# Block inverses of a gated DeltaNet layer: their TensorE products in four pieces, head products planned in pieces of two channel blocks

## The chip, the cores and the metric

The kernel runs on one core of one Trainium2 chip. The metric is the time of one execution in microseconds (us), lower is better; a row of times gives the median of several executions.

## What is computed

A two-layer backbone over 512 latent tokens and 256 context tokens of width 1024, in float32. Layer 0 is a bidirectional gated DeltaNet, layer 1 a grouped-query attention with axial rotary angles. The change lies in layer 0 alone. Its reference, cut to what matters here:

```python
p = u @ w_in                                    # u: normed and modulated tokens
qkv = silu(centred_dwconv(p[..., :4096], conv_w))   # 8 q heads, 8 k heads, 16 v heads of 128
...                                             # q and k l2-normalised; beta = sigmoid, g = log-decay
# per head and direction, in chunks of 64 tokens:
a = where(strict, einsum('bhncd,bhnsd->bhncs', kb, kc) * decay, 0)
t_inv = triangular_solve(eye + a, eye, left_side=True, lower=True, unit_diagonal=True)
u = t_inv @ vb;  w = t_inv @ (kb * exp(gc))
def step(s, xs):                                # scan over the chunks
    v_new = u_i - w_i @ s
    o = qd_i @ s + qk_i @ v_new
    s = s * gl_i + kd_i^T @ v_new
```

## The kernel before

Layer 0 has two stages that matter here. In the first, TensorE (PE) makes the projections of the heads and, between them, the chunk matrices; in the second it runs the scan over twelve steps.

*Head products.* The first stage handles 40 column blocks of `w_in` in the order of `heads` ("qz" eight times, then "vvz" eight times), 128 columns each. Each block is a weight tile of 8 channel blocks (`KT`) of 128x128, split into a high and a low float32r half (`high` on ScalarE, `low` on GpSimd or VectorE). `products_of(n_, part)` makes 24 matmuls for one block: 8 channel blocks by three passes (high weight by high input, high by low, low by high), into one PSUM bank `g`; part 0 has the 512 latent tokens, part 1 the 256 context tokens. These matmuls are line 752 (756 after the change). VectorE and ScalarE then make the convolution and the SiLU of each part.

*Chunk matrices.* Tokens are kept as six pairs of chunks, t = 0 to 5. For each t the plan holds: `masked_nodes` (matrix of k with itself, masked and decayed, PE line 948); `solve_nodes`, in which GpSimd (POOL) inverts the 32x32 diagonal blocks of two t at once in 31 steps (lines 1051, 1052, and 1055 at the end); `join_nodes`, which joins two 32x32 inverses to one 64x64 inverse; and `query_nodes` (q by k, PE line 1014, masked, decayed by POOL on line 634, stored to `qk_d`).

*The join, for one t.* VectorE transposes the solved blocks into two tiles `U0` and `U1` (line 1073). `first` makes 64 float32 matmuls of 32x32 by 32 columns into the PSUM tile `pp` (line 1080). `negated` copies `pp` with a minus sign over `mo` on ScalarE (line 1083). `second` makes 64 more such matmuls into `pw` (line 1090). Eight copies `gathered` (`Tt` from `U`) and four copies `placed` (`Tt` from `pw`) fill a 1 MB tile `Tt`, which is stored to `t_d` (line 1111). Each of the 64 matmuls shows as two MATMUL and two LDWEIGHTS records in the profile, so a burst is "x128".

*What sets the order.* Every piece of work is a `Node` with an engine ("T" is TensorE, "V" VectorE, "S" ScalarE, "G" GpSimd, "D" a transfer or a delay), a cost, a rank, the nodes it depends on (`deps`), and the buffers that it takes with those that free them (`takes`, sizes in `RINGS`). `in_order` takes, again and again, the node that can start first by its own clock of each engine, and of several the one of lowest rank. The nodes are then run in that order, and each engine executes its own instructions in just that order. A "T" node depending on another engine's node is placed at least `LAG["T"]` = 1.0 after it; on a "D" node no engine clock acts. Transfers are issued on SyncE's queue (SP) in order as well.

*Loads of the scan's first step.* At the end of the list, `first_kq`, `first_v`, `first_T`, `first_QK` and `first_kt` load what step 0 reads: `ckq` (line 605), `cv` (1155), `cT` (1161), `cQK` (1167, 1169) and `ckt` (1180); after the change these lines are 605, 1177, 1183, 1189, 1191 and 1202. `cT`, `cQK` and `ckt` take the three tiles `df` that the decays used. The loads of the next steps (same tile names, other numbers) stand behind them on SP. In the scan, `products` makes `ks` (PE line 1460; VectorE's `r` on line 1463 reads `ks` and `cv`), `solve` makes `pr` from `r` and `cT` (1485), `update` makes `pq` from `cQK` (1507) and `su` from `ckt` (1515).

Of the kernel before, what the change touches and what calls it, by code (L numbers as in the profile page):

```python
# [8 lines left out]
F32 = mybir.dt.float32  # L9
# [8 lines left out]
P = 128  # L18
D = 1024
KT = 8  # L20
NLAT, NCTX = 512, 256
NTOK = NLAT + NCTX
NT = 6
QH, VH = 8, 16
# [73 lines left out]
def backbone(tc, a, out):  # L98
    nc = tc.nc
    V, S, G, T = nc.vector, nc.scalar, nc.gpsimd, nc.tensor  # L100
# [93 lines left out]
    pa = psA.__enter__()  # L194
# [281 lines left out]
    p2, p5 = gemm_T(None, None, 64, "ab")  # L476
# [187 lines left out]
    def node(engine, cost, rank, fn, *deps, takes=()):  # L664

        x = Node(engine, cost, rank, fn, deps, list(takes))
        nodes.append(x)
        return x
# [73 lines left out]
        weights[n_][2] = ap_.tile([P, KT, P], F32R, tag="wl", name=f"wl_{n_}", bufs=3)  # L742
        (G if n_ < EARLY else V).tensor_tensor(weights[n_][2], weights[n_][0], weights[n_][1], ALU.subtract)  # L743

    def products_of(n_, part):

        c0, n = parts[part]
        w, wh, wl = weights[n_]
        ps = pa.tile([P, 512], F32, tag="g", name=f"g{n}_{n_}", bufs=4)
        for k in range(KT):  # L750
            for m, (w_, u) in enumerate(((wh, uh), (wh, ul), (wl, uh))):
                T.matmul(ps[:, :n], w_[:, k], u[:, k, c0:c0 + n], start=k == 0 and m == 0, stop=k == KT - 1 and m == 2)  # L752
        sums[n_, part] = ps

    def taken(n_, part):

# [92 lines left out]
    for n_, (f_, h) in enumerate(heads):  # L849
# [4 lines left out]
        lw = node("D", 0.0 if first else 5.5, n_, go(load_weights, n_))  # L854
        hi = node("S", 0.0 if first else 1.06, n_ + 0.5, go(high, n_), lw)
        lo = node("G" if n_ < EARLY else "V", 0.0 if first else 2.5 if n_ < EARLY else 1.6, n_ + 0.5, go(low, n_), hi)
        for part in range(2):
            p[part] = node("T", (5.48, 2.92)[part], n_, go(products_of, n_, part), lo, p[0], *before)
            before = [p[part]]
        lw.takes.append(("w", [lo]))  # L860
        hi.takes.append(("wh", [p[1]]))
        lo.takes.append(("wl", [p[1]]))
        for part in range(2):
            if f_ == "z":
                th = node("S", (0.62, 0.4)[part], n_, go(tanh_of, n_, part), p[part], s_[0])
                s_[part] = node("V", (0.69, 0.42)[part], n_, go(silu_of, n_, part), th)
                if part == 0:
                    alloc = th
            else:
                x = first_ = node("S", (0.7, 0.48)[part], n_, go(taken, n_, part), p[part], acc0 if part else None)  # L870
                if part == 0:
                    acc0 = x
                for j in (0, 1, 3, 4):
                    x = node("V", (0.75, 0.49)[part], n_, go(spread, n_, part, j), x)
                th = node("S", (0.62, 0.4)[part], n_, go(tanh_of, n_, part), x)
                s_[part] = node("V", ((0.83, 0.56) if f_ == "q" else (0.69, 0.42))[part], n_, go(silu_of, n_, part), th, s_[0])
                if part == 0:
                    alloc = s_[0]
            p[part].takes.append(("g", [s_[part]]))
        if f_ != "z":  # L880
            acc0.takes.append(("acc", [s_[1]]))
        if f_ == "v":
# [181 lines left out]
    def join_nodes(t, rank):  # L1064
# [7 lines left out]
            U = box[d] = tl.tile([P, 2, VH, 32], F32, tag=f"U{d}", name=f"U{d}" + nm)  # L1072
            V.transpose(U.rearrange("p v h j -> p j (v h)"), X if d == 0 else X.rearrange("p i j -> p j i"))

        def first():
            box["pp"] = pp = pa.tile([P, VH, 32], F32, tag="gq", name="pp" + nm)
            for h in range(VH):
                for b in range(4):
                    i0, o0, d = b * 32, (b ^ 1) * 32, 1 - b % 2
                    T.matmul(pp[o0:o0 + 32, h, :], mos[t][i0:i0 + 32, h, :], box[d][i0:i0 + 32, of(b, d), h, :], start=True, stop=True, tile_position=(i0, o0))  # L1080
# [1 line left out]
        def negated():  # L1082
            S.activation(mos[t], box["pp"], AF.Copy, scale=-1.0)

        def second():
            box["pw"] = pw = pa.tile([P, VH, 32], F32, tag="gq", name="pw" + nm)
            for h in range(VH):
                for b in range(4):
                    i0 = b * 32
                    T.matmul(pw[i0:i0 + 32, h, :], box[1 - b % 2][i0:i0 + 32, of(b, b % 2), h, :], mos[t][i0:i0 + 32, h, :], start=True, stop=True, tile_position=(i0, i0))  # L1090
# [8 lines left out]
        def placed(b):  # L1099
            c0 = 32 - (b % 2) * 32  # L1100
            S.copy(Tt[b * 32:b * 32 + 32, of(b, b % 2), :, c0:c0 + 32], box["pw"][b * 32:b * 32 + 32])

        us = []
        for d in range(2):
            us.append(node("V", 2.15, rank, lambda d=d: turned(d), solved[t], before_U.get(t), *us))
        p1 = node("T", 1.32, 0, first, *us)
        sn = node("S", 0.61, rank - 0.5, negated, p1)
        p2 = node("T", 1.32, 0, second, sn)
        gs = [node("S" if t < LATE else "G", 0.62 if t < LATE else 1.1, rank, lambda b=b, d=d: gathered(b, d), us[d], cleared) for d in range(2) for b in range(4)]
        pl = [node("S", 0.58, rank - 0.5, lambda b=b: placed(b), p2) for b in range(4)]  # L1110
        st_ = node("D", 6.0, rank, lambda: dma(t_d[t], Tt), *gs, *pl)
        p1.takes.append(("gq", [sn]))
        p2.takes.append(("gq", pl))
        us[0].takes.append(("U", gs + [p2]))
# [5 lines left out]
        u_done[t], second_done[t] = us, p2  # L1120

    def clear():

# [1261 lines left out]
```

## Time and profile before

| what | value |
|---|---|
| median of 3 executions | 1182.38 us (1180.96 to 1186.59) |
| the profiled execution, its own time | 1193.88 us |
| its span (first to last instruction) | 1192.1 us, 28134 instructions |
| PE busy | 1134.5 us, 95% |
| VectorE, ScalarE, GpSimd busy | 836.9, 705.8 and 631.4 us |
| head products, line 752 | 222.0 + 217.7 + 217.1 us over 1920 matmuls |
| `pp` and `pw` matmuls | 768 records each, 192 ns median |
| first `pp`, last `pw` | 349.5 and 561.3 us |
| scan, first `ks` | 565.14 us |

The profiled execution took 11.5 us more than the median of the ordinary ones. Times in the trace are us from the span's start. A row of a timeline gives the start, the duration, the engine and line, the output and inputs, and in brackets the idle time before it with what ended it. Durations of matmuls include their way through the array, so the spacing of starts is what one costs in a stream. "issue" is time in which the engine waited for nothing that the profile shows.

### The profile page before, as it was taken

The numbers are of one execution on the slowest core, as the hardware profiler recorded it, in microseconds if no ns is written. First come the engines' busy times: TensorE is split into PE (matmuls) and PEld (weight loads), VectorE is DVE, ScalarE is ACT, GpSimd is POOL, SyncE is SP. The second block draws the span as 40 slices with busy tenths as digits, with TensorE's granted clock in tenths as the row PEclk, the third lists the DMA queues.
The fourth block names the chain that finished last, engine by engine and source line by source line (L and its number), as shares of the span: only waits on it lengthen the run. The fifth ranks groups of instructions, "written<-read, shape, count | busy, mean of one in ns | idle before, by whom it ended". The sixth has DMA issues, their size and how long they took to land.

```text
span 1192.1 us, 28134 instructions
## 1 busy us (share of the span) xinstructions
PE 1134.5 (95%) x10779; PEld 921.5 (77%) x10779; DVE 836.9 (70%) x1842; ACT 705.8 (59%) x1831; POOL 631.4 (53%) x515
## 2 busy tenths in 40 slices
PE   3999999999998999999999999999998989999996
PEld 1777678888887888888566666788886878989885
DVE  2498664778889687777678888687667866556536
ACT  5544344677666668655779888653533246666632
POOL 0031014329999899793575598557663043153531
PEclk9999999999999999999999999999999999999999
DMA  9478977555646585785988856576743021121133
GB/s 320 167 229 243 305 238 207 152 170 143 175 118 206 186 237 176 238 255 172 276 225 243 248 155 172 169 228 191 234 159 124 1 71 36 37 71 37 40 131 77
DMA packets 166104, 204.56 MB, mean 172 GB/s; under 512 B 13489, under 2 KB 115026, under 8 KB 165202
## 3 DMA queue, kind: packets, MB, share of 16 engines
q1 hardware_dynamic: 159170, 199.13, 55.0%
q10 hardware_dynamic: 6800, 3.64, 1.0%
q8 instruction: 85, 1.39, 0.5%
q14 instruction: 49, 0.40, 0.1%
HBM read 161.96 MB, written 40.67 MB: 170 GB/s over the span
## 4 chain that ended last, share of the span: by engine, by line
PE 82%; DVE 6%; DMA 6%; ACT 2%; issue 2%; SPq 1%; POOL 1%; ACTq 0%; DVEq 0%; POOLq 0%
PE g L752 29%; PE po L1385 11%; PE ks L1460 6%; PE pg L2026 3%; PE pg L1980 3%; PE g_k L414 3%; PE po L2094 2%; DMA aw<-in_ada_w 2%; PE kv L1833 2%; PE su L1515 2%; PE s L2044 2%; PE pso L2327 2%; PE pr L1485 2%; PE pa L245 1%; PE pt L2072 1%
## 5 line engine op out<-in xcount | busy, mean ns | idle before, releaser
L752 PE MATMUL g<-uh,wh 128*128 128x512 f32 (+1 forms) x640 | 222.0, 347 | 0.0
L752 PE MATMUL g<-ul,wh 128*128 128x512 f32 (+1 forms) x640 | 217.7, 340 | 3.9 <-issue 3.9
L752 PE MATMUL g<-uh,wl 128*128 128x512 f32 (+1 forms) x640 | 217.1, 339 | 0.0
L769 DVE SCALAR_TENSOR_TENSOR acc<-g,cwv,acc 128x510 f32<-128x510 f32 (+1 forms) x192 | 117.0, 614 | 43.7 <-ACT acc L761 39.2
L752 PEld LDWEIGHTS g<-uh,wl 128*128 128x128 f32 x640 | 122.8, 192 | 17.4 <-issue 4.2
L752 PEld LDWEIGHTS g<-uh,wh 128*128 128x128 f32 x640 | 122.8, 192 | 14.6 <-issue 1.1
L752 PEld LDWEIGHTS g<-ul,wh 128*128 128x128 f32 x640 | 123.0, 192 | 12.5 <-issue 0.5
L1385 PE MATMUL po<-woh,y 128*128 128x512 f32 x384 | 127.7, 400 | 0.0
L1468 POOL TENSOR_TENSOR S<-S,glb 128x512 f32<-128x512 f32 x88 | 89.9, 1041 | 58.1 <-PE ks L1460 58.1
L1052 POOL TENSOR_TENSOR X<-X,tmp 128x62 f32<-128x62 f32 (+15 forms) x93 | 95.6, 1028 | 7.3
L1051 POOL TENSOR_TENSOR tmp<-L,X 128x62 f32<-128x62 f32 (+15 forms) x93 | 94.6, 1018 | 6.4
L1460 PE MATMUL ks<-S,ckq 128*64 128x256 f32 x768 | 93.5, 386 | 2.3 <-ACT O L1465 2.2
L1385 PEld LDWEIGHTS po<-woh,y 128*128 128x128 f32 x384 | 72.2, 188 | 14.8 <-issue 0.2
L1460 PEld LDWEIGHTS ks<-S,ckq 128*64 128x64 f32 x768 | 51.1, 137 | 41.5 <-ACT O L1465 10.4
L1328 POOL TENSOR_TENSOR wol<-wo,woh 128x512 fp32r<-128x512 f32 (+1 forms) x32 | 52.6, 1643 | 56.2 <-ACT woh L1319 25.5
L1385 PE MATMUL po<-wol,y 128*128 128x512 f32 x192 | 75.1, 391 | 0.0
L743 POOL TENSOR_TENSOR wl<-w,wh 128x1024 fp32r<-128x1024 f32 x11 | 26.4, 2399 | 90.5 <-ACT wh L738 72.8
L211 POOL TENSOR_TENSOR wl_k<-w_k,wh_k 128x1024 fp32r<-128x1024 f32 x8 | 19.0, 2386 | 99.2 <-ACT wh_k L210 99.2
L761 ACT ACTIVATE acc<-g,cwv 128x512 f32<-128x512 f32 (+1 forms) x48 | 27.9, 581 | 64.2 <-PE g L752 63.7
L2075 DVE TENSOR_TENSOR pT<-pt,pT 128x384 fp32r<-128x384 f32 x64 | 33.4, 554 | 45.4 <-ACT pT L2074 45.4
L1463 DVE SCALAR_TENSOR_TENSOR r<-ks,negV,cv 128x128 f32<-128x128 f32 x192 | 56.6, 345 | 7.2 <-PE ks L1460 3.6
L1533 DVE TENSOR_TENSOR S<-su,S 128x512 f32<-128x512 f32 x88 | 56.6, 685 | 5.7 <-PE su L1515 3.9
(416 smaller groups left out, 2887.8 us busy)
## 6 DMA issues: line engine op xcount, KB each, us to landing
aw<-in_ada_w SPq DMA_DIRECT2D x24, 1024.0 KB, 7.5
w<-in_dn_w_in SPq DMA_DIRECT2D x40, 512.0 KB, 4.9
wo<-in_dn_w_out SPq DMA_DIRECT2D x32, 512.0 KB, 3.9
cv<-v_d SPq DMA_DIRECT2D x80, 128.0 KB, 5.5
df<-gc_d SPq DMA_DIRECT2D x48, 128.0 KB, 3.5
z_d<-sil SPq DMA_DIRECT2D x16, 384.0 KB, 4.3
v_d<-vt SPq DMA_DIRECT2D x16, 384.0 KB, 4.2
t_d<-Tt SPq DMA_DIRECT2D x6, 1024.0 KB, 4.7
```

The lines of the kernel that those rows point to most:

```text
L414: mm = T.matmul(pg_[:m, :n], w[:, k, :m], u[:, k, c0:c0 + n], start=k == 0 and n_ == 0, stop=k == KT - 1 and n_ == 2)
L752: T.matmul(ps[:, :n], w_[:, k], u[:, k, c0:c0 + n], start=k == 0 and m == 0, stop=k == KT - 1 and m == 2)
L769: V.scalar_tensor_tensor(a_[:, c0 + lo:c0 + hi], ps[:, lo + j - 2:hi + j - 2], cwv[:, j, ct:ct + 1], a_[:, c0 + lo:c0 + hi], ALU.mult, ALU ...
L1051: G.tensor_tensor(tv, bcast(L[:, :, j + 1:, j], 3, j + 1), bcast(X[:, :, j, 0:j + 1], 2, n), ALU.mult)
L1052: G.tensor_tensor(X[:, :, j + 1:, 0:j + 1], X[:, :, j + 1:, 0:j + 1], tv, ALU.subtract)
L1328: G.tensor_tensor(wl[:, :c], w[:, :c], wh[:, :c], ALU.subtract)
L1385: T.matmul(acc[j][nh], y[i][:, j, :], ww[k][:, nh * 512:(nh + 1) * 512], start=h == 0 and x == 0, stop=h == VH - 1 and x == 2)
L1460: T.matmul(ks[r0:r0 + 64, w], kq[:, w, slot(hh), r0:r0 + 64], St[hh][:, d], start=True, stop=True)
L1463: V.scalar_tensor_tensor(r[:, 2 * j + i], ks[:, 0, i], negV[:, visit, t, h0 + i:h0 + i + 1], v[:, 2 * hh + i], ALU.mult, ALU.add)
L1468: G.tensor_tensor(St[hh], St[hh], bcast(g_, 3, P), ALU.mult)
L1533: V.tensor_tensor(St[hh], raw(sj, 0, [[512 - 1024 * j, 2], [P, 2], [1, P]]), St[hh], ALU.add)
L1980: T.matmul(pgq, uL[i][:, k, t * P:(t + 1) * P], wq[j][:, k], start=k == 0 and n_ == 0, stop=k == KT - 1 and n_ == 2)
```

## The change

`products_of` is planned in four pieces per part, two channel blocks each (six matmuls), so that other "T" nodes can be placed between pieces; the PSUM bank is taken by the first piece and freed as before. For t below `LATE` = 4, `first` and `second` of a join become four pieces of 16 matmuls each, with a "D" node of cost `APART` = 0.3 between them; for t = 4 and 5 the four pieces are one node as before. All joins get rank 20 (t = 2 and 3 had 1025 and 1035). The query products of t = 5 get rank 1091 instead of 1150, ahead of those of t = 0 to 4.

```diff
-    def products_of(n_, part):
+    PIECES = 4
+
+    def products_of(n_, part, i):
...
-        ps = pa.tile([P, 512], F32, tag="g", name=f"g{n}_{n_}", bufs=4)
-        for k in range(KT):
+        if i == 0:
+            sums[n_, part] = pa.tile([P, 512], F32, tag="g", name=f"g{n}_{n_}", bufs=4)
+        ps = sums[n_, part]
+        for k in range(i * KT // PIECES, (i + 1) * KT // PIECES):
...
+        opened = []
         for part in range(2):
-            p[part] = node("T", (5.48, 2.92)[part], n_, go(products_of, n_, part), lo, p[0], *before)
-            before = [p[part]]
+            for i in range(PIECES):
+                p[part] = node("T", (5.48, 2.92)[part] / PIECES, n_, go(products_of, n_, part, i), lo, p[0], *before)
+                before = [p[part]]
+                if i == 0:
+                    opened.append(p[part])
...
-            for h in range(VH):
+            for h in range(i * VH // 4, (i + 1) * VH // 4):
...
-        p1 = node("T", 1.32, 0, first, *us)
-        sn = node("S", 0.61, rank - 0.5, negated, p1)
-        p2 = node("T", 1.32, 0, second, sn)
+        def in_pieces(fn, *deps):
+            xs, last = [], None
+            if t >= LATE:
+                last = node("T", 1.32, 0, lambda: [fn(i) for i in range(4)], *deps)
+                return last, last
+            for i in range(4):
+                rest = node("D", APART, 0, lambda: None, last) if last else None
+                last = node("T", 0.33, 0, lambda i=i: fn(i), *deps, rest)
+                xs.append(last)
+            return xs[0], last
+
+        p1, p1_ = in_pieces(first, *us)
+        sn = node("S", 0.61, rank - 0.5, negated, p1_)
+        p2, p2_ = in_pieces(second, sn)
...
-    LATE = 4
+    LATE, APART = 4, 0.3
...
-        join_nodes(t, 20 if t // 2 != 1 else 1005 + 10 * t)
+        join_nodes(t, 20)
     for t in range(NT):
-        query_nodes(t, 1100 + 10 * t)
+        query_nodes(t, 1100 + 10 * t if t < NT - 1 else 1091)
```

What this makes of the instruction order is shown at three places; line numbers above 742 shift by up to 22.

First, PE at the join of t = 1, during the products of block 22. Before (`pp` is one run of 64 matmuls, alternating between the two `U` tiles):

```order
L752 MATMUL g_22_4353<-ul,wh_4098 128x512
L752 MATMUL g_22_4353<-uh,wl_4119 128x512
L1080 MATMUL pp_4401<-U_1_4384,mo_2578 32x32
L1080 MATMUL pp_4401<-U_1_4349,mo_2578 32x32
...
L752 MATMUL g_22_4474<-uh,wh_4098 128x256
L752 MATMUL g_22_4474<-ul,wh_4098 128x256
```

And after:

```order
L756 MATMUL g_22_4365<-uh,wl_4131 128x512
L1089 MATMUL pp_4414<-U_1_4385,mo_2577 32x32
L1089 MATMUL pp_4414<-U_1_4363,mo_2577 32x32
...
L756 MATMUL g_22_4432<-uh,wh_4055 128x256
L756 MATMUL g_22_4432<-ul,wh_4055 128x256
...
L1089 MATMUL pp_4414<-U_1_4385,mo_2577 32x32
```

After 16 matmuls of `pp` there are now, in most places, 12 head products before the next 16. Over the whole first stage PE goes back to head products after something else 72 times, where it was 45.

Second, PE at the join of t = 4. Before, it stands in block 37, with transposes and a whole part 1 of products (24) between `pp` and `pw`:

```order
L752 MATMUL g_37_6455<-uh,wl_6282 128x512
L1080 MATMUL pp_6502<-U_4_6440,mo_3577 32x32
...
L463 MATMUL tr_v_6571<-ident,sil_6406 128x128 x4
L463 MATMUL tr_v_6572<-ident,sil_6406 128x128 x2
L752 MATMUL g_37_6581<-uh,wh_6257 128x256
...
L1090 MATMUL pw_6624<-mo_3577,U_4_6440 32x32
```

After, it stands in block 35, and `pp` and `pw` are still whole bursts:

```order
L756 MATMUL g_35_6216<-uh,wl_6060 128x512
L1089 MATMUL pp_6230<-U_4_6194,mo_3589 32x32
...
L756 MATMUL g_35_6216<-uh,wh_6025 128x512
...
L1101 MATMUL pw_6320<-mo_3589,U_4_6194 32x32
L1101 MATMUL pw_6320<-mo_3589,U_4_6166 32x32
```

The join of t = 4 moved ahead by two blocks, and between its two bursts there are 12 products now.

Third, SP where the scan's loads begin. Numbers of tiles: `ckt_6772` and `ckt_7014` are of step 0 in the kernel before and after, `cv_6447` and `cv_6197` too; 7237 to 7241 are of step 1 in both. Before:

```order
L1180 DMA ckt_6772<-kt_d 64x512 x4
L827 DMA v_d_70<-vt_6882 128x6x128
L1111 DMA t_d<-Tt_1780 128x2048
L827 DMA v_d_70<-vt_7015 128x6x128
L809 DMA z_d<-sil_6961 128x768
L605 DMA ckq_7237<-k_d 128x1024
L605 DMA ckq_7237<-q_d 128x1024
L1161 DMA cT_7240<-t_d 128x1024
L1155 DMA cv_6447<-v_d_70 64x512 x2
L1155 DMA cv_7239<-v_d_67 64x512 x2
```

After:

```order
L1041 DMA qk_d<-df1q_6824 128x1024
L1191 DMA cQK_6948<-qk_d 64x512
L605 DMA ckq_7237<-k_d 128x1024
L605 DMA ckq_7237<-q_d 128x1024
L1183 DMA cT_7240<-t_d 128x1024
L1177 DMA cv_7239<-v_d_67 64x512
L1202 DMA ckt_7014<-kt_d 64x512 x4
L830 DMA v_d_70<-vt_7005 128x6x128
L1177 DMA cv_7239<-v_d_67 64x512
L1177 DMA cv_7239<-v_d_68 64x512
L812 DMA z_d<-sil_6968 128x768
L1177 DMA cv_7239<-v_d_68 64x512
```

Step 1's loads of `ckq` and `cT` moved ahead of step 0's load of `ckt` and of the last v store, the last store of `t_d` is earlier (eight rows above this piece), and `ckt` now stands behind the last store to `qk_d`, whose tile it takes over. The last piece of step 0's `cv` stands seven rows below the v store that it reads (before: five).

More of the change, by code (lines that the diff above doesn't have):

```diff
@@ L743, in low @@
         (G if n_ < EARLY else V).tensor_tensor(weights[n_][2], weights[n_][0], weights[n_][1], ALU.subtract)
-    def products_of(n_, part):
+    PIECES = 4
+    def products_of(n_, part, i):
         c0, n = parts[part]
         w, wh, wl = weights[n_]
-        ps = pa.tile([P, 512], F32, tag="g", name=f"g{n}_{n_}", bufs=4)
-        for k in range(KT):
+        if i == 0:
+            sums[n_, part] = pa.tile([P, 512], F32, tag="g", name=f"g{n}_{n_}", bufs=4)
+        ps = sums[n_, part]
+        for k in range(i * KT // PIECES, (i + 1) * KT // PIECES):
             for m, (w_, u) in enumerate(((wh, uh), (wh, ul), (wl, uh))):
                 T.matmul(ps[:, :n], w_[:, k], u[:, k, c0:c0 + n], start=k == 0 and m == 0, stop=k == KT - 1 and m == 2)
-        sums[n_, part] = ps
     def taken(n_, part):
@@ L878, in backbone @@
                     alloc = s_[0]
-            p[part].takes.append(("g", [s_[part]]))
+            opened[part].takes.append(("g", [s_[part]]))
         if f_ != "z":
@@ L1073, in turned, with first @@
             V.transpose(U.rearrange("p v h j -> p j (v h)"), X if d == 0 else X.rearrange("p i j -> p j i"))
-        def first():
-            box["pp"] = pp = pa.tile([P, VH, 32], F32, tag="gq", name="pp" + nm)
-            for h in range(VH):
+        def first(i):
+            if i == 0:
+                box["pp"] = pa.tile([P, VH, 32], F32, tag="gq", name="pp" + nm)
+            pp = box["pp"]
+            for h in range(i * VH // 4, (i + 1) * VH // 4):
                 for b in range(4):
@@ L1083, in negated, with second @@
             S.activation(mos[t], box["pp"], AF.Copy, scale=-1.0)
-        def second():
-            box["pw"] = pw = pa.tile([P, VH, 32], F32, tag="gq", name="pw" + nm)
-            for h in range(VH):
+        def second(i):
+            if i == 0:
+                box["pw"] = pa.tile([P, VH, 32], F32, tag="gq", name="pw" + nm)
+            pw = box["pw"]
+            for h in range(i * VH // 4, (i + 1) * VH // 4):
                 for b in range(4):
@@ L1105, in join_nodes @@
             us.append(node("V", 2.15, rank, lambda d=d: turned(d), solved[t], before_U.get(t), *us))
-        p1 = node("T", 1.32, 0, first, *us)
-        sn = node("S", 0.61, rank - 0.5, negated, p1)
-        p2 = node("T", 1.32, 0, second, sn)
+        def in_pieces(fn, *deps):
[11 more added lines that the diff above has]
+        p2, p2_ = in_pieces(second, sn)
         gs = [node("S" if t < LATE else "G", 0.62 if t < LATE else 1.1, rank, lambda b=b, d=d: gathered(b, d), us[d], cleared) for d in range(2) for b in range(4)]
-        pl = [node("S", 0.58, rank - 0.5, lambda b=b: placed(b), p2) for b in range(4)]
+        pl = [node("S", 0.58, rank - 0.5, lambda b=b: placed(b), p2_) for b in range(4)]
         st_ = node("D", 6.0, rank, lambda: dma(t_d[t], Tt), *gs, *pl)
@@ L1113, in join_nodes @@
         p2.takes.append(("gq", pl))
-        us[0].takes.append(("U", gs + [p2]))
+        us[0].takes.append(("U", gs + [p2_]))
         if t >= 2:
@@ L1119, in join_nodes @@
         before_U[t + 1] = us[1]
-        u_done[t], second_done[t] = us, p2
+        u_done[t], second_done[t] = us, p2_
     def clear():
```

## The prediction

> **What bounds the kernel now.** I read the table of stretches first, then the chain that ended last around the stretches that stand out. In the first stage of layer 0 PE is full: it goes from one product to the next without a gap, so no engine but PE sets the end there, and moving work on the others is worth nothing. Three stretches between 380 and 610 us break this (columns: PE, weight loads, VectorE, ScalarE, GpSimd busy, then PE's granted clock, DMA share, GB/s):
>
> ```profile
> 375.00:380.00 5.00, 5.00 (x24) 4.13 (x23) 5.00 (x4) 4.89 (x9) 4.76 (x4) 1.00 0.85 288
> 380.00:385.00 5.00, 2.05 (x132) 1.57 (x131) 4.96 (x4) 3.95 (x8) 4.76 (x4) 0.93 0.99 342
> 385.00:390.00 5.00, 4.05 (x20) 4.05 (x20) 4.12 (x5) 0.00 (x0) 4.69 (x5) 0.50 0.99 260
> 480.00:485.00 5.00, 2.53 (x103) 2.06 (x93) 4.57 (x6) 2.57 (x5) 4.70 (x4) 0.83 0.94 316
> 485.00:490.00 5.00, 5.00 (x20) 4.04 (x19) 2.23 (x2) 3.39 (x8) 1.78 (x2) 0.83 0.47 112
> 600.00:605.00 5.00, 3.05 (x47) 2.39 (x47) 1.73 (x6) 2.56 (x9) 3.16 (x3) 0.78 0.99 295
> 605.00:610.00 5.00, 5.00 (x78) 2.90 (x72) 3.36 (x8) 2.27 (x8) 2.54 (x3) 0.88 0.77 222
> ```
>
> The first two stops come at the bursts of the block inverses, and the chain there names no other engine, only "issue" (start, duration, what):
>
> ```profile
> 375.06 5.46 PE g L752 x24
> 380.52 1.22 PE pp L1080 x82
> 382.05 3.90 issue
> 385.95 5.07 PE g L752 x23
> ...
> 475.36 1.22 PE pp L1080 x82
> 479.63 0.53 PE pw L1090 x41
> 480.17 2.47 issue
> 482.64 0.97 PE pw L1090 x57
> 483.61 7.14 PE g L752 x24
> ```
>
> A burst of 128 matmul and 128 weight-load records passes in 1.22 us. PE's instructions come by a DMA queue of their own, and around the first stop the data queue fills the engines:
>
> ```profile
> q8 instruction: 85, 1.39, 0.5%
> ...
> 376.68 0.34 SPq L1111 DMA_DIRECT2D t_d<-Tt  x1
> 378.54 0.32 SPq L605 DMA_DIRECT2D ckq<-k_d  x1
> 378.91 1.25 SPq L605 DMA_DIRECT2D ckq<-q_d  x1
> 380.25 0.49 SPq L733 DMA_DIRECT2D w<-in_dn_w_in  x1
> ...
> q1 hardware_dynamic: 378, 1.76, 97.0%
> ...
> q8 instruction: 1, 0.02, 2.3%
> ```
>
> The first row is the whole span: 85 packets, 1.39 MB, so 16 KB each; 2 x 10779 records over 85 packets are 254 a packet. One burst, 256 records, therefore eats one packet in 1.22 us, where a block of 24 products, 48 records, takes 5.46 us. The last two rows are two windows: from 376.5 to 382 only data moved, at 97% of all engines; from 381.9 to 384.6 one instruction packet came, within the stop. So I read the stops as PE having run out of instructions, behind 2.5 MB that SP had just issued (t_d 1 MB, ckq twice 0.5, w 0.5).
>
> The Trainium skill's Runtime: NRT & Kernel Launch, section Instruction fetch mechanics, has blocks of 256 instructions fetched ahead by a queue of the engine's own, and calls the cost of crossing a block mostly hidden. The 254 records agree; the 3.90 us of "issue" do not agree with hidden.
>
> **The change, part by part.**
>
> *The two stops.* The first costs 3.90 idle; 23 products of 256 columns then take 5.07 where 23 x 0.12 = 2.76 (spacing below) would do, since the clock is 0.50: 2.31 more. 6.2 in all. The second costs 2.47, the split burst 0.53 + 0.97 - 1.22 = 0.28, and 24 products 7.14 - 5.46 = 1.68: 4.4 in all. Together 10.6 us. In pieces, 64 records pass in 0.31 us, then 12 products (24 records) in 1.4 (256 columns) to 2.7 us (half of 5.46), so 256 records last some 6 to 10 us instead of 1.22. The first stop ended 385.95 - 380.52 = 5.4 us after its burst began, the second 482.64 - 475.36 = 7.3 us after its first burst. So these stops should go or shrink below 1 us at t = 0 to 3.
>
> *Going in and out.* Each time PE leaves the products and comes back costs a little at both ends:
>
> ```profile
> 447.39 0.28 PE L752 MATMUL g<-ul,wh 128*128 128x256 f32 x1
> 447.51 0.28 PE L752 MATMUL g<-uh,wl 128*128 128x256 f32 x1
> 447.72 1.29 PE L1080 MATMUL pp<-U,mo 32*32 32x32 f32 x128
> 448.94 0.50 PE L752 MATMUL g<-uh,wh 128*128 128x512 f32 x1
> 449.28 0.40 PE L752 MATMUL g<-ul,wh 128*128 128x512 f32 x1
> 449.51 0.40 PE L752 MATMUL g<-uh,wl 128*128 128x512 f32 x1
> ```
>
> In: 0.21 instead of 0.12, so 0.09. Out: 0.34 instead of 0.23, so 0.11. The order has 72 returns to products instead of 45: 27 x 0.20 = +5.4 us, all on PE, which is full, so nothing hides it. The bounds: 0 if small runs overlap better than long ones, 27 x 0.4 = 10.8 if a run of 0.31 us also waits for its own weights; I take 5.4, measured on the same two neighbours.
>
> *The bursts left whole, t = 4 and 5.* The order puts 12 products (2.7 us) between `pp` and `pw` of t = 4, where there were transposes and 24 products of part 1:
>
> ```profile
> 526.56 4.13 DVE L1073 STREAM_TRANSPOSE U<-X 128x1024 f32<-128x1024 f32 x2
> 538.10 1.09 PE L1080 MATMUL pp<-U,mo 32*32 32x32 f32 x106
> ```
>
> 512 records in 1.22 + 2.7 + 1.22 = 5.1 us is two packets; the second stop stood at just such a pair, 475.36 and 479.63, 4.3 us apart. And the order has step 0's `cv` loads just ahead. Of twelve bursts before, two stopped, so four whole ones give two thirds of a stop at 4.4: +2.9. Bounds: 0, and 6.2 + 4.4 = 10.6 for two. The wait for `U` is no new term: before, it was ready at 530.7 and used at 538.1; the planner now leaves it less, and I bound that at 0 to 2 us and put it in this range.
>
> *The start of the scan.* SP's loads stand in another order there:
>
> ```profile
> 553.51 3.13 SPq L1180 DMA_DIRECT2D ckt<-kt_d  x4
> 566.78 1.15 SPq L605 DMA_DIRECT2D ckq<-k_d  x1
> 569.79 3.95 SPq L1155 DMA_DIRECT2D cv<-v_d  x6
> ...
> 570.28 8.01 DMA cv<-v_d
> 597.45 4.99 DMA cT<-t_d
> ...
> 565.14 1.95 PE L1460 MATMUL ks<-S,ckq 128*64 128x256 f32 x16
> 579.80 1.95 PE L1460 MATMUL ks<-S,ckq 128*64 128x256 f32 x16 [1.54 <-ACT O L1465]
> 602.57 1.00 PE L1485 MATMUL pr<-r,cT 64*64 64x128 f32 x16 [1.95 <-DMA cT<-t_d]
> ```
>
> SP issues without a pause from 566 on, and step 2's `cT` gets its turn only at 597.45, 32 us after the scan's start; PE waits 1.95 for it, and the clock of 0.78 and 0.88 over 10 us costs 5 x 0.22 + 5 x 0.12 = 1.7: 3.6 in all. After the change step 1's `ckq` and `cT` are issued before the scan instead of 1.6 us after its start, so SP's queue runs ahead by some us and this wait should go: -3.6. The 1.54 behind `cv` I leave: its store and load keep their places to each other. In exchange `ckt` of step 0, issued 11.6 us before the scan before, now stands behind the last `qk_d` store; PE needs it some 8 us into the scan. If late: 0 to +4 (a load's 8.01 against that slack), and SP with all behind it waits too. I take 0. Bounds of this part: -5.1 to +4.
>
> Earlier transposes, `gathered` and `placed` copies on ScalarE and VectorE, the earlier query of t = 5, and shorter waits for products on all engines lie beside a full PE: nothing, as long as PE never waits for them.
>
> **The sum.** Against the profiled execution (1193.88 us): -10.6 + 5.4 + 2.9 - 3.6 = -5.9. But that execution took 11.5 us more than the median of the ordinary ones, about the size of its two stops. What packet a burst falls on and which transfers run beside it is the same in every execution, so I keep the stops, at three quarters (between half and all) of their size: 8.0. Then -8.0 + 5.4 + 2.9 - 3.6 = -3.3, and 1182.4 - 3.3 = **1179.1 us**. This measurement tells about 0.5% (5.9 us) from no change, so the forecast is no change that can be told.
>
> **The rivals.**
>
> *The whole gain.* The ordinary executions have the stops in full and the whole bursts never stop: -10.6 + 5.4 - 3.6 = -8.8, 1173.6; with the 1.54 gone too, 1172. For it: the three ordinary times spread by 5.6 us, the size of one stop. Against: the profiled execution is far above all three. Chance 0.28.
>
> *The stops belong to the profiled execution alone.* Then there is nothing to win in the first stage: +5.4, with 0 to -3.6 at the scan, 1184 to 1188. For it: 11.5 against 10.6. It decides once less than half of 10.6 stands in ordinary executions. Chance 0.15.
>
> *New stops at the whole bursts.* At t = 4 the pair is closer than the pair of the second stop and next to the `cv` loads. One stop of 6.2 and one of 4.4, or one and a late `ckt`: -8.0 + 5.4 + 10.6 - 3.6 = +4.4, 1186.8; without the gain at the scan 1190.4, slower. It decides when PE has more than one such stop. Chance 0.14.
>
> *The stops are not the instruction queue.* A cause that cutting does not touch would leave both where they are, and only the switches would count: +5.4, 1187.8. For it: the name "issue" is only the absence of a cause. Against: a packet arrives inside the stop. Chance 0.06. That is also what follows if fetching is mostly hidden, as the Trainium skill's Runtime: NRT & Kernel Launch (Instruction fetch mechanics) has it.
>
> **The numbers.** The forecast, 1175 to 1183, has the other 0.37. Over 5.9 us faster (below 1176.5): the whole gain 0.27, a tenth of the forecast's range, in all 0.32. Slower (above 1188.3): half of the new stops, a third of the last rival, and a little of the second: 0.12. The rest, 0.56, within. Eight in ten: 1171 to 1189, which takes in the whole gain (1172) and one rival of the other sign short of its worst.
>
> **What would show it.** Right: no "issue" beside `pp` and `pw` at t = 0 to 3 and a clock of 1.00 there; pieces of 32 matmul records with 0.09 and 0.11 around them; the first `ks` at 565.1 - 10.6 + 5.4 + 2.9, near 563; no wait for `cT` near 35 us into the scan. Wrong: an "issue" of over 2 us at the whole bursts of t = 4 or 5, a wait of `su` for `ckt` in the scan's first 10 us, PE waiting for `U` ahead of a `pp`, or a median below 1173 or above 1188.

## The result, and the profile after

| what | before | after |
|---|---|---|
| median (9 executions each) | 1185.77 us | 1191.04 us |
| lowest and highest | 1180.96 to 1190.94 | 1188.19 to 1194.62 |
| ratio after / before | | 1.0055, 95% interval 1.0036 to 1.0073 |
| the profiled execution | 1193.88 us | 1188.19 us |

The change makes the kernel 5.3 us slower by the medians (4.3 to 8.7 by the interval). The two profiled executions alone would say the opposite: that of before was longer than any of its nine timed ones, that of after is the shortest of its nine. Further measurements of before gave medians of 1184.5 to 1186.2 us, so the 1182.38 of three executions stood some 2 to 4 us too low. One later execution of before ran at a granted clock of 0.75 throughout and took 1412 us; it is in no median and no ratio here.

What the change was to do in the first stage of layer 0, it did. The stretches of after at the two old stops and at the scan's start (PE, weight loads, VectorE, ScalarE, GpSimd busy, PE's granted clock, DMA share, GB/s):

```profile
380.00:385.00 5.00, 5.00 (x54) 3.95 (x53) 4.96 (x6) 4.91 (x9) 4.76 (x4) 1.00 0.93 304
385.00:390.00 5.00, 5.00 (x93) 4.43 (x93) 4.89 (x6) 3.69 (x6) 4.84 (x5) 1.00 1.00 331
480.00:485.00 5.00, 5.00 (x35) 4.61 (x34) 3.06 (x5) 2.87 (x8) 4.84 (x5) 1.00 0.82 263
580.00:585.00 5.00, 3.19 (x20) 1.60 (x24) 3.53 (x10) 3.47 (x11) 1.04 (x1) 0.74 0.74 231
```

At 380 to 390 the DMA engines are as full as before (shares 0.93 and 1.00 against 0.99), yet PE is busy throughout and its clock is 1.00 where it was 0.93 and 0.50. The chain there, and at the whole bursts of t = 5:

```profile
384.27 0.38 PE pp L1089 x32
384.66 1.62 PE g L756 x12
386.28 0.38 PE pp L1089 x32
...
543.63 0.55 PE pw L1101 x42
544.18 1.12 issue
545.31 0.89 PE pw L1101 x58
```

One stop of 1.12 us is left, inside the whole `pw` of t = 5, and the clock stays at 1.00 behind it. The price stands at each piece (start, duration):

```profile
377.13 0.28 PE L756 MATMUL g<-ul,wh 128*128 128x256 f32 x1
377.25 0.28 PE L756 MATMUL g<-uh,wl 128*128 128x256 f32 x1
377.46 0.45 PE L1101 MATMUL pw<-mo,U 32*32 32x32 f32 x32
377.85 0.38 PE L756 MATMUL g<-uh,wh 128*128 128x256 f32 x1
378.07 0.28 PE L756 MATMUL g<-ul,wh 128*128 128x256 f32 x1
```

Going in takes 0.21 us instead of 0.12. The piece itself takes 0.39, where a quarter of a burst of 1.22 is 0.305. Coming out, the second product starts 0.22 behind the first instead of 0.12. Together that is 0.09 + 0.08 + 0.10, so 0.27 to 0.28 for each return to the products.

The scan starts worse than before. SP's row of the last store of `v` in before, then SP's rows and the waits of PE in after:

```profile
564.83 0.37 SPq L827 DMA_DIRECT2D v_d<-vt  x1
```

```profile
560.50 0.33 SPq L1041 DMA_DIRECT2D qk_d<-df1q  x1
...
563.62 0.45 SPq L1177 DMA_DIRECT2D cv<-v_d  x1
564.71 2.44 SPq L1202 DMA_DIRECT2D ckt<-kt_d  x4
567.31 0.47 SPq L830 DMA_DIRECT2D v_d<-vt  x1
568.67 2.94 SPq L1177 DMA_DIRECT2D cv<-v_d  x2
...
575.32 1.23 SPq L1177 DMA_DIRECT2D cv<-v_d  x2
...
PE ks L1482 <- ACT O L1487: 4.1, 2, 3.5
```

Before, that store was issued 0.3 us ahead of the first `ks` (565.14), and step 0's `cv` could be loaded from 569.79 on. After, it is issued 1.7 us behind the first `ks` (565.6): SP held 0.6 us at the four `ckt` loads until the `qk_d` store issued at 560.50 had landed, and issuing them took 2.44 us more. ScalarE had written `vt` by 564.9, so the store stood 2.4 us for SP alone. The row at 563.62 loads step 1's `cv`, as do three more behind it. The two at 568.67 hold SP until step 1's `ckq` and `cT` have landed, 2.9 us in all. Step 0's `cv` is the pair at 575.32, 9.7 us behind the first `ks` instead of 4.65; the store had landed at 573.8. PE waits 3.50 us ahead of the scan's fifth group of 16 `ks` (before 1.54), with a clock of 0.74 in that stretch. The wait for `cT` at 602 is gone.

### The profile page after: what moved, and what is told of

It reads as the page before. It is cut to its first block, busy times and chain, and to the rows that moved or that the text cites. A ratio compares the mean times of both kernels' runs of the same rounds, so it can differ in the third digit from the quotient of the medians.

```text
span 1186.3 us, 28121 instructions
## 1 busy us (share of the span) xinstructions
PE 1139.0 (96%) x10779; PEld 917.5 (77%) x10779; DVE 827.0 (70%) x1842; ACT 706.1 (60%) x1831; POOL 632.5 (53%) x515
## 4 chain that ended last, share of the span: by engine, by line
PE 85%; DVE 6%; DMA 3%; SPq 2%; ACT 2%; POOL 1%; issue 1%; ACTq 0%; DVEq 0%; POOLq 0%
PE g L756 29%; PE po L1407 11%; PE ks L1482 7%; PE pg L2048 3%; PE pg L2002 3%; PE g_k L414 3%; PE su L1537 3%; PE po L2116 2%; PE kv L1855 2%; PE s L2066 2%; PE pr L1507 2%; PE pso L2349 2%; PE pa L245 2%; PE pq L1529 2%; PE pt L2094 1%; PE pso L2135 1%
## 5 line engine op out<-in xcount | busy, mean ns | idle before, releaser
L1059 POOL TENSOR_TENSOR X<-X,tmp 128x62 f32<-128x62 f32 (+15 forms) x93 | 99.0, 1065 | 7.3
L1058 POOL TENSOR_TENSOR tmp<-L,X 128x62 f32<-128x62 f32 (+15 forms) x93 | 90.7, 975 | 6.5
L2121 POOL TENSOR_TENSOR yT<-ay,yT 128x256 fp32r<-128x256 f32 x16 | 11.8, 737 | 89.9 <-ACT yT L2120 89.9
```

Source lines behind the costliest of these rows:

```text
L1058: G.tensor_tensor(tv, bcast(L[:, :, j + 1:, j], 3, j + 1), bcast(X[:, :, j, 0:j + 1], 2, n), ALU.mult)
L1059: G.tensor_tensor(X[:, :, j + 1:, 0:j + 1], X[:, :, j + 1:, 0:j + 1], tv, ALU.subtract)
```

## The experiments

Rows of one kernel's first and last instruction give the lengths used below: the first stage runs from the first `g` to the first `ks`, the scan from there to the last `ks`. For the changed kernel (columns: duration min, median, max in ns; first and last start in us):

```profile
L1482 PE MATMUL ks<-S,ckq x768: 379/379/631, 565.6 to 747.5; 128*64 128x256 f32 x192
L756 PE MATMUL g<-uh,wh x640: 277/388/798, 165.6 to 565.1; 128*128 128x512 f32 x80, 128*128 128x256 f32 x80
```

That is 400.0 us and 181.9. Without its stop of 1.12 the stage is 398.8; that of before, 401.4, is 390.8 without its 10.6.

Theory A, after the result: PE does run out of instructions at whole bursts and the cut cures it, but 27 returns cost 0.30 us each instead of 0.20, and the rest is the scan's start. Rivals: the stops never cost ordinary executions anything; the new ranks cost the time and not the pieces; planning the products in pieces costs it.

**Before, once more.** No edit; what two copies of one kernel differ by.

> The kernel before, unchanged, as a control and as a second profile of it. Time 1.000 of before within its noise. Theory A (the change costs 0.30 us for each return of PE to head products, and the stops at the bursts are a matter of chance): first product to first scan matmul 390.8 us plus whatever stops fall into it (the first profile: 401.4 with 10.6 of stops); here fewer or other stops than in the first profile, 0 to 2 of them. Rival B (the stops stand in every execution, and the change lost its gain elsewhere): again stops of 6.2 and 4.4 us at t = 1 and t = 3, 401 us.

Measured: 1185.76 against 1186.21, ratio 0.9997 (0.9971 to 1.0022). Its question about the stops is answered by the profiles of before further below.

**Bursts whole.** The changed kernel, no join cut:

```diff
-            if t >= LATE:
+            if t >= 0:
```

> The changed kernel with the two bursts of every join left whole (t = 0 to 5); head products still planned in pieces, ranks as changed. PE returns to head products 53 times instead of 72. Theory A (0.30 us per return): first stage without stops 398.8 - 19 x 0.30 = 393.1 us, time about 5 us below the changed kernel and 1 to 3 above the one before. Rival C (the ranks and the loads at the start of the scan cost the time, not the cutting): as the changed kernel, 398.8 and 1.0055 of before, and a stop of about 3.5 us at the fifth ks.

Measured: 1191.08, ratio 1.0045 (1.0021 to 1.0069): as slow as with the cut. The stage is 400.4 us, and stops are back, if short: 1.10 inside `pw` of t = 1 and 1.46 behind that of t = 3. Two waits are of a kind that neither theory had, 1.19 for VectorE's `KQ1q` and 2.3 for its `sil`, the latter with 3.4 us of half clock. Without all these 392.6, for 8 more returns than before. The expected time was missed by some 5 us: the stops and waits of the first stage ate what the fewer switches saved, and the scan's start waits 3.58 here too.

**Eight pieces.** `VH // 4` becomes `VH // 8`, eight nodes of 0.165.

> The changed kernel with the bursts of t = 0 to 3 cut into eight pieces instead of four. PE returns to head products 94 times instead of 72. Theory A (0.30 us per return): first stage without stops 398.8 + 22 x 0.30 = 405.4 us, time 1.011 of before. If a return costs 0.20, as predicted: 403.2. Rival C (ranks and loads): as the changed kernel, 398.8 and 1.0055.

Measured: 1237.85, ratio 1.0433 (1.0396 to 1.0469). The planner no longer gets the last joins and queries done before the head products end: the last product starts at 564.9 and the first `ks` only at 591.9, and PE then waits 10.2 us for `cT`, 8.1 for `ckt`. It says nothing on a single switch.

**Old ranks.** The changed kernel with the ranks of before:

```diff
-        join_nodes(t, 20)
+        join_nodes(t, 20 if t // 2 != 1 else 1005 + 10 * t)
...
-        query_nodes(t, 1100 + 10 * t if t < NT - 1 else 1091)
+        query_nodes(t, 1100 + 10 * t)
```

> The changed kernel with the ranks of the joins and of the queries as before; pieces kept. 69 returns to head products. Theory A: first stage without stops 390.8 + 24 x 0.30 = 398.0 us, time 1.005 of before, the start of the scan as before the change (1.5 us behind cv, 2.0 behind step 2's cT). Rival C (ranks and loads cost the time): time as before, 1.000 to 1.002.

Measured: 1204.05, ratio 1.0155 (1.0118 to 1.0192). The first stage, 398.5 us and no stop in it, agrees with A (69 returns, 24 more). The loss is in the scan, 197.0 us:

```profile
PE su L1537 <- DMA ckt<-kt_d: 7.9, 1, 7.9
...
PE pq L1529 <- DMA cQK<-qk_d: 2.6, 2, 2.1
```

PE also waits 4.64 us ahead of the second group of `ks`. So with joins in pieces the new ranks do better than the old: without them the scan's first loads come late.

**The new ranks alone, on the kernel before** (the last diff, reversed, on before).

> The kernel before with the changed ranks alone (joins of t = 2 and 3 at 20, the last query at 1091): bursts and products whole, 45 returns to products as before. Theory A, the pieces pay by their switches (0.30 us a return) and the ranks only decide when the scan's loads are issued: no more switches, the last store of v stands ahead of step 1's loads as before, so the first stage lasts 390.8 us without its stops and the time stays within 3 us of before, 1183 to 1189. Rival B, the ranks themselves cost the 5 us: 1190 to 1193, with a wait behind cv of over 3 us at the scan's start.

Measured: 1191.00, ratio 1.0054 (1.0031 to 1.0077). A expected 1183 to 1189 and missed; the rival was right that the ranks cost as much by themselves, with no switch more. Its first stage is no longer than that of before, 398.2 us (391.4 without stops and half clock); its scan is 184.3 us, with 4.83 us of wait behind `cv`. The chain:

```profile
565.72 5.24 DMA v_d<-vt
...
571.54 7.89 DMA cv<-v_d
```

The store of `v` goes out at 565.72, 2.5 us behind the first `ks` (563.25), after four `ckt` loads of 3.14 us, though `vt` was ready at 562.9.

**The products in pieces alone** (old ranks, bursts whole).

> The changed kernel with its head products planned in four pieces, but the bursts whole and the ranks as before: 49 returns to products. A: 390.8 + 4 x 0.30 = 392.0 us for the first stage without stops, and since the order has the last store of v behind some of step 1's loads, a wait behind cv of 3 to 4 us at the scan's start as in the changed kernel: 1187 to 1192. Rival C, planning the products in pieces costs nothing by itself: within 2 us of before, 1184 to 1188. Rival D, the old ranks with products in pieces push the joins past the products as they did with cut bursts: over 1198.

Measured: 1190.82, ratio 1.0043 (1.0021 to 1.0065), inside A's range. But the profiled execution took 1186.3, with 400.1 us in the first stage (stops of 0.70 to 1.63 at four places and 2.2 us of waiting for `sil`) and only 0.62 behind `cv`. So the wait behind `cv`, where A put the cost, is not there. This execution is 4.5 us below the median and shows no loss against before; where the others lose is not shown.

**The store of v ahead of step 1's loads.** The changed kernel; `v_stores` collects what `store_v` issues:

```diff
-            if p == 0:
+            if p == 0 and s == 1:
+                with tc.issue_after(v_stores[-1]):
+                    load_step(s)
+            elif p == 0:
                 load_step(s)
```

> The changed kernel with step 1's loads issued behind the last head's store of v instead of ahead of it; nothing else moves. A: the store goes out some 2 us earlier and with less beside it, so the wait behind cv falls from 4.1 us to between 0.5 and 2 and the half clock behind it goes (1.7 us): 1191.0 - 2.6 - 1.7, near 1187, or 1189 if PE then waits for cT some 35 us into the scan as it did before. Rival: the wait comes from the product's end and not from the loads in front, then the time stays at 1191 and the wait at 4.

Measured: 1188.05, ratio to before 1.0018 (0.9997 to 1.0039). That is 3.0 us below 1191.04, or 4.4 by the two ratios. The wait behind `cv` is 2.11 us with no half clock (A said 0.5 to 2), 0.42 for `cT`. The store itself still stands behind `ckt`, 1.4 us behind the first `ks`; what has gone from in front of step 0's `cv` are the waits of step 1's.

**The first 128 products of each burst twice**, on the kernel before:

```diff
-            for h in range(VH):
+            for h in [*range(VH), *range(VH)]:
```

> The kernel before with the first 128 products of each block inverse made twice in a row (same result): 512 records instead of 256 at six places. The extra work is 6 x 1.22 = 7.3 us on a full PE. If PE's instructions run out at such bursts (A), 512 records in 2.44 us eat two packets, and where 2 to 3 MB of data move beside them each of t = 0 to 3 stops for 2 to 4 us and drops the clock for 1 to 2 us more: 1186 + 7.3 + 8 to 16, that is 1201 to 1209, with issue rows inside or right behind pp. Rival, instruction fetch is hidden in ordinary executions: 1186 + 7.3 = 1193.5.

Measured: 1224.0, ratio 1.0320 (1.0294 to 1.0347). The work added is 7.3 us; 39 came. Every one of the six double bursts stops (waits of PE, then the chain at t = 0 and t = 1):

```profile
PE pp L1080 <- issue: 19.6, 6, 5.7
...
351.90 0.47 PE pp L1080 x23
352.38 4.03 issue
...
387.98 1.22 PE pp L1080 x82
389.19 2.36 issue
...
393.14 2.69 issue
```

The stops are 22.2 us in the first stage, which lasts 429.6 us. 24 us of it are at half clock, 4.3 of these inside stops. Without the stops and half of the other 19.6 it has 397.6, near the 390.8 of before and the 7.3 added. The rival, fetches that are hidden, expected 1193.5.

**The same doubled products, in pieces.** The changed kernel, each of the four pieces of `first` made twice:

> The changed kernel with each piece of the first 128 products made twice in a row: the same 12 x 128 products and 6 x 128 more as in the kernel that doubled them uncut (1224.0), but in pieces of 128 records with head products between at t = 0 to 3. A (PE runs out only where too many instructions pass too fast): 398.8 + 7.3 us for the stage plus some 2.5 at each of the two whole doubled bursts, clock 1.00 to 530: 1191 + 7.3 + 4, near 1202. Rival (what counts is the number of records, not how close they stand): stops at each t as uncut, 1220 or more.

Measured: 1211.84, ratio 1.0231 (1.0195 to 1.0266). The same number of products, 12 us less. The stage is 414.5 us against 429.6 uncut, 406.3 without its waits: 398.8 + 7.5. At t = 0 to 3 one stop of over half a microsecond is left; the two long ones, 2.50 and 3.39, are in the whole double bursts at t = 4 and 5. The short one and the first long one:

```profile
387.28 0.56 issue
...
517.99 1.57 PE pp L1089 x93
519.56 2.50 issue
```

What counts is how closely the records stand. The time is 10 us above the 1202 that was expected, in part by the scan's start (4.83 behind `cv` in the profile); the rest is not accounted for.

**Two pieces, with the store of v first** (and step 1's `cv` behind step 0's).

> The changed kernel with bursts cut in two instead of four, step 1's loads issued behind the last store of v, and step 1's cv behind step 0's: 61 returns to products instead of 72. A: the first stage lasts 390.8 + 16 x 0.30 = 395.6 us plus stops of at most 2 us, the wait behind cv 0.5 to 2 us: 11 x 0.30 = 3.3 below the changed kernel with its loads behind the store (1188.05), near 1184.8, no slower than before. Rival: half a burst (128 records in 0.61 us) still empties PE's queue, then stops of 1 to 3 us at t = 0 to 3 give the 3.3 back: 1188 to 1190.

Measured: 1191.79, ratio 1.0053 (1.0023 to 1.0084): slower even than the rival's 1188 to 1190, and not by its cause. The stage is 402.4 us, 395.3 without stops, near A's 395.6, and the halves at t = 0 to 3 stop for 0.77 us at the most. The long stop is in the whole `pw` of t = 4, 18 products behind its whole `pp`, and the wait behind `cv` is 3.62:

```profile
508.71 2.34 PE g L756 x18
511.05 1.08 PE pw L1103 x74
512.13 3.61 issue
```

**The ranks with step 1's cv behind step 0's**, on before.

> The kernel before with the new ranks, and step 1's cv issued behind step 0's cv. A: the 6 us that the ranks cost alone are the order of SP's loads at the scan's start: the wait behind cv falls from 4.83 us with 6.8 us of half clock to 0.5 to 2 us, 1191.0 - 2.8 - 3.4, that is 1184 to 1187. Rival: the ranks cost in the first stage (the joins of t = 2 and 3 fall on another place of PE's queue and stop): the time stays at 1190 to 1192, with a first stage of over 398 us.

Measured: 1189.36, ratio 1.0035 (1.0006 to 1.0065). The time is 1.6 us below that of the ranks alone, not 4 to 7, and the two intervals overlap. The store still stands behind `ckt` (2.5 us behind the first `ks`), and the wait was 5.37. `cv` was issued as soon as that store had landed (569.4), so its place among the loads was not what made it late here.

**The load of ckt behind that store.** As the store first, and `load_kt` moved from `first_kt` into `load_step(0)`:

```diff
+                with tc.issue_after(v_stores[-1]):
+                    load_kt(first_set["kt"], 0)
                 load_rows(first_set["v"][:, 12:16], v_d[3], t)
```

> The changed kernel with step 0's ckt and step 1's loads issued behind the last head's store of v. A: the store goes out within 0.5 us of the first ks instead of 1.7 us after it, so the wait behind cv falls from 3.50 and 4.30 to 0 to 1 us and its half clock goes: 1191 - 3.5 - 1.7, that is 1184.5 to 1187. Rival: ckt itself or step 1's loads now come late (PE waits for ckt near 573 or for ckq or cT near 581): 1189 to 1192.

Measured: 1187.45, ratio 1.0032 (1.0009 to 1.0056), the upper end of A's range. The store goes out 0.66 us ahead of the first `ks` (565.56), `cv` is issued 2.9 us behind it, and the wait for it is gone; the 0.52 us left behind `ACT O` come one group of `ks` later, for step 1's `cv`:

```profile
564.90 0.38 SPq L832 DMA_DIRECT2D v_d<-vt  x1
565.38 1.91 SPq L1204 DMA_DIRECT2D ckt<-kt_d  x3
...
568.44 1.25 SPq L1179 DMA_DIRECT2D cv<-v_d  x2
...
PE pr L1513 <- DMA cT<-t_d: 3.7, 1, 3.7
PE ks L1488 <- ACT O L1493: 1.1, 2, 0.6
```

In its place, in the profiled execution (1197.08 us, the longest of its twelve), PE waits 3.7 us for step 2's `cT`: the rival named a late `cT`, though of step 1.

**The same move on before with the new ranks.**

> The kernel before with the new ranks, and the same move of step 0's ckt behind the last store of v. A: the ranks' 6 us are this load in front of that store (2.5 us late in the two profiles with the new ranks): the wait behind cv falls from 4.83 to 0 to 1.5 us, the half clock goes, 1183 to 1186, as before. Rival: 1189 to 1192, the ranks cost elsewhere.

Measured: 1188.94, ratio 1.0054 (1.0031 to 1.0076); A's 1183 to 1186 missed. The store does go out 0.3 us ahead of the first `ks` (561.46 against 561.77), but the four `ckt` loads and step 1's `ckq` and `cT` stand between it and `cv`, which is issued from 568.16 on, 6.4 us behind the first `ks`; the wait is 4.34.

**Only t = 1 in pieces**, with the load of `ckt` behind the store.

> As kt_late, but only the bursts of t = 1 in four pieces, all others whole: 57 returns. A: the first stage is 390.8 + 12 x 0.30 = 394.4 us plus 0 to 4.4 for a stop at t = 2 or 3, no stop near 386; with a wait behind cv of under 1 us 1180 to 1186, no slower than before. Rival: the stops move to the next whole bursts in full, stage over 400, 1187 to 1191.

Measured: 1200.34, ratio 1.0121 (1.0083 to 1.0159), worse than either side said. No stop stands near 386 any more, but the stage is 403.6 us: a stop of 1.84 behind the whole bursts of t = 3, one of 1.79 inside `pw` of t = 4, and another wait, behind t = 2:

```profile
430.63 0.61 ACT Tt L1108
...
431.27 0.61 ACT g L787
...
431.90 0.70 DVE sil L799
...
432.65 2.31 PE g L756 x6
```

ScalarE has the twelve copies of a join, with one other operation between, ahead of a head's own work, and PE waits 2.7 us for it. Another 3.6 goes on `cT` in the scan. The profile also has 611.8 us outside the two stages, where the four of before have 605.6 on the mean; no cause of that is shown.

**Before and after, three and one more profiles**, unchanged.

> The kernel before, unchanged, for a second profile. If the stops at the bursts are the same in every execution, as the prediction had it, 3.90 us at 386 and 2.47 at 483 stand there again, with a first stage near 401. If they depend on what else moves at that moment (A), the places stay within a burst or two and the sizes do not: anything from 0 to 4 us each, and the half clock behind them only where one is over 2 us; the total time then follows, 1180 to 1192.

> The changed kernel, unchanged, for a second profile. A: the first stage is 398.8 us plus stops of 0 to 2 us at the whole bursts of t = 4 and 5, clock 1.00 up to 540; the wait behind cv 3 to 5 us with 3.4 to 6.8 us of half clock. If the 3.50 of the first profile was a single execution's, it falls below 2 here.

> The kernel before, for a third profile. If an ordinary execution loses less at the bursts than the two profiled ones (A), one of 1181 to 1186 us has a first stage of 394 to 399 us instead of 401.4, and a wait at the scan's start of under 2 us. If the first stage is 401 here too, the bursts cost the same in every execution, and the difference to the median lies behind the scan (the gap near 905 us, 0.9 to 5 us so far).

> The same as the third profile, once more: the first stage against the time of the execution. A expects the stage to differ by some us between executions, and the time with it; the rival expects 401 in all four.

| profile | time | first stage | scan | wait behind `cv` |
|---|---|---|---|---|
| before, third | 1180.25 | 396.3 | 177.7 | 0.4 |
| before, fourth | 1183.52 | 397.9 | 179.4 | 0.87 |
| before, second | 1187.60 | 401.4 | 179.4 | 0.79 |
| before, first | 1193.88 | 401.4 | 182.4 | 1.54 |
| after, first | 1188.19 | 400.0 | 181.9 | 3.50 |
| after, second | 1190.49 | 399.8 | 182.7 | 4.30 |

The third and fourth ran on one chip, the second on another. The place of the first stop is the same in all four of before, right behind `pp` of t = 1, after one head product; its size is 2.17, 3.25, 4.34 and 3.90 us. The third and the fourth:

```profile
381.64 1.22 PE pp L1080 x82
382.86 0.32 PE g L752
383.18 2.17 issue
385.34 2.91 PE g L752 x23
```

```profile
381.34 1.22 PE pp L1080 x82
382.55 0.32 PE g L752
382.87 3.25 issue
386.12 4.39 PE g L752 x23
```

The 2.17 leaves the clock alone (23 products in 2.91, 0.127 each), the 3.25 halves it (4.39, 1.6 more). So the stop is no accident of one execution, but its cost is. Without stops and waits of over 0.3 us, and without what the half clock adds outside them, the first stage takes 390.7, 392.1, 391.9 and 391.9 us (391.6 on the mean) in the first to fourth profile; it loses 10.7, 9.3, 4.4 and 6.0. In the two of after the stop stands at one place and the stage varies by 0.2 us.

What the stops are can be read from the packet records of the traces. The instruction queue `q8` brings 85 packets; where the doubled kernels have 6 x 256 PE records more, it brings 91, so a packet holds 256 of PE's instructions. In 19 profiles of these kernels the first stage has 46 stops of over 0.3 us named "issue". At each of them, the number of records that PE had run (matmuls, weight loads and its waits) is 256 times the packets landed by its end, plus 193 or 194, and each ended 1.3 to 1.7 us after a packet had landed. None of the 15 waits there that name an engine or a transfer stands at such a count. So PE stops at the end of a packet and goes on a nearly fixed time after the next has landed. By the same count, no packet of before starts to move while PE has more than some 300 instructions left. From there it needs 0.9 us to move and 1.3 more, while a burst runs 256 instructions in 1.22: by this estimate a whole burst can empty the queue even where no other transfer is in the way. The size follows the packet's start: in the first stop of before it began 0.2 us ahead of the stop, then 1.0, 1.4 and 2.0 us into it, where the stops are 2.17, 3.25, 3.90 and 4.34. That data transfers make it start later is argued from a DMA share of 0.99 there, and not shown.

## Why the prediction was wrong

The difference forecast was -3.3 us; it is +5.3. The time, 1191.04, lies 2 us above the range.

*The stops: the cause right, the size right for the mean only.* The prediction kept them at three quarters, 8.0 us. The four profiles of before have 391.6 us of work on the mean and a first stage of 399.2, so they lose 7.6; the two on either side of the timed median (1183.52 and 1187.60) lose 6.0 and 9.3. The sentence that packet and transfers are "the same in every execution" is half wrong: the packet is, the delay is not. That three quarters came so near the mean is luck. The Trainium skill's Runtime: NRT & Kernel Launch (Instruction fetch mechanics) has the crossing of a 256-instruction block mostly hidden. The doubled bursts disagree, with 22.2 us of stops at six joins where 512 records stand in a row. The rival of a cause that cutting does not touch falls with them: in pieces, the same records stop for 0.56 us at t = 0 to 3.

*The switches: mis-sized.* 27 returns were put at 0.20, 5.4 us. The stage without stops went from 390.7 to 392.1 up to 398.8, that is 0.25 to 0.30 each, 7.2 on the mean. The term that was missing is the piece's own end: a burst of 1.22 us holds it once, and four pieces pay it four times (0.39 for a quarter instead of 0.305). 8, 16 and 24 more returns, measured in the kernels with whole bursts, with half bursts and with the old ranks, gave 392.6, 395.3 and 398.5.

*The whole bursts: over-sized.* 2.9 was put in; 1.12 and 1.03 stand in the two profiles.

The first stage so comes out at -7.6 + 7.2 + 1.1 = +0.7 us against a forecast of -8.0 + 5.4 + 2.9 = +0.3: wrong sizes that cancel, which is luck.

*The scan's start: the step that failed.* Forecast -3.6; by the profiles the scan went from 179.7 (mean of four) to 182.3 (of two), +2.6: 6.2 us of the 8.6 by which the forecast missed. That `cT` would come in time was right, but its 3.6 were those of one profile: in the four of before PE waits 1.95, 1.26, 0 and 1.14 us for it, and only the first has half clock there, so it was worth 1.5 on the mean. Wrong was that the store and load of `cv` "keep their places to each other": `ckt`, whose shift behind the last `qk_d` store the prediction had named and put at 0, holds SP until that store has landed and takes 2.4 us to issue, with the store of `v` behind it, and step 1's loads, now ahead of step 0's `cv`, hold SP again. The wait behind `cv` grew from 0.9 us (mean of four) to 3.9, with 3.4 us of half clock. Moving loads behind that store brought it to 2.1 us and to none, and the time to 1188.05 and 1187.45. The ratio of the first (up to 1.0039) and that of the change (from 1.0036) barely touch; that of the second overlaps it, with 3.7 us of waiting for `cT` in its profile. How the wait grows can be read from when step 0's last `cv` lands. In the four profiles of before that is 12.1 to 13.2 us behind the first `ks`, for waits of 0.4 to 1.5. In after it is 14.7 and 15.5, for 3.5 and 4.3; with the ranks alone 16.2 for 4.8; with the store first 13.3 for 2.1. In these, and in four more kernels (bursts whole, halves, and the new ranks with the loads of `cv` or `ckt` moved), the wait is the landing less 11.2 to 11.7 us. The doubled products in pieces fall outside (17.1 for 4.8), since PE had waited for `ckt` there before. When the load is issued does not tell it alone: after 9.7 us it landed in 4.3, where in before it took about 8.

*What stays open.* Stage and scan give +0.7 + 2.6 = 3.3 of the 5.3 us. Outside these two stages before takes 604.5 to 608.2 us and after 604.4 and 606.0, so nothing is lost there by the profiles; the spread is mostly one gap near 905 us, 0.9 to 5 us in different executions of the same kernel. It is not of the kind above: PE's count of records stands 141 to 149 above a whole number of packets there, not at 193, and its cause is not known. The two profiled executions of after lie 1.7 us on the mean below its median, so some 2 us are of executions that no profile shows. Why the products in pieces alone cost 6 us in the median, while their profiled execution was short, is open too, and so is what the new ranks cost beside a late `cv`: no order of the loads that was tried brought them back to the time of before.

*The rivals.* "New stops at the whole bursts" came nearest in time (1186.8 to 1190.4), by a mechanism that gave 1.1 us. "The stops belong to the profiled execution alone" (1184 to 1188) is wrong as a cause: all four profiles of before have them. The base was too low as well: with 1185.8 instead of 1182.4 the same sum would have given 1182.5.

No version beat the kernel before. The nearest, the changed kernel with step 1's loads behind the last store of `v` (ratio 1.0018, 0.9997 to 1.0039), cannot be told from it.

## What to carry to other kernels

Count what a cut adds at both ends and inside: a piece of a burst costs its share plus its own end, here some 0.27 us for every return to a full PE, so 27 more returns must save over 7 us before they pay. A profiled stop is to be weighed by several profiles, since its place may be fixed and its size not. When a load is moved on an in-order queue, look for what it waits for there and which store stands behind it; four loads that waited for another store here helped to delay the one store that the next stage needed.

## What the runs showed of the hardware

128 matmuls and 128 weight loads of 32x32 in 1.22 us let PE run dry for 0.5 to 4.3 us at two or three of the twelve bursts of before, the first time always at the same instruction. Twice as many in 2.44 us did so at each of six joins, for 2.4 to 5.7 us, also at t = 4 and 5. In pieces of a quarter with 12 head products between, the records of t = 0 to 3 passed without a stop of over 0.3 us. PE stopped at the end of a packet of 256 instructions and went on 1.3 to 1.7 us after the next had landed, in all 46 stops.

An idle time of 3.25 us halved PE's clock, one of 1.12 left it at 1.00. Near 2 us the length alone does not tell: 2.14, 2.29 and 2.47 us halved it; 2.17, 2.42 and 2.52 did not. The half clock lasted 3.41 or 6.83 us each time in before and after. The Trainium skill's TensorE: Matmul & The Clock Gate (Part 1: The HAM clock gate) puts the return to full clock at about 3.4 us of sustained work. The 23 products after the 3.25 agree, at 1.6 us longer than at full clock: 3.4 us at half speed lose 1.7.
